# One decoder block on one core: other early transfers and ranks, a stored order, and the scores' low-part product on 64 rows

## The chip, the cores and the metric

The kernel runs on one core of one Trainium2 chip. Its time is the device time in microseconds (us) of one execution of the program, given as the median of several. Five engines share the work: TensorE (PE, with its weight load PEld shown apart), VectorE (DVE), ScalarE (ACT), GpSimd (POOL) and SyncE (SP), which here issues every DMA.

## The reference

One decoder block on x of 256 tokens by 1024 features, with 256 memory tokens, all in float32:

```python
h = rmsnorm(x, g_pre_mix); z = h @ w_in
q_nsa, kv_nsa, g_nsa, qkv_ml, if_ml, o_ml, q_mem, g_merge = split(z)
# 1 sparse attention: 16 heads of 64 in 4 groups of 4 that share keys and values
o_cmp, p_cmp = nsa_compressed(...)      # keys of 32-token blocks through a small MLP
o_slc = nsa_selected(...)               # top 16 blocks of 64 keys: at 256 tokens all four
o_win = nsa_window(...)                 # window of 512: at 256 tokens plain causal attention
y_nsa = gb[0] * o_cmp + gb[1] * o_slc + gb[2] * o_win
# 2 mLSTM, 4 heads of 128, with a causal convolution
y_ml = sigmoid(o_ml) * headnorm(mlstm_chunkwise(q_m, k_m, v_m, i_pre, logf))
# 3 cross-attention to the memory, 4 heads of 128
y_mem = memory_xattn(q_mem, mem, g_mem, w_mem_kv)
y = sum(sigmoid(g_merge[b]) * (y_b @ w_proj_b))
x = x + rmsnorm(y @ w_out, g_post_mix)
x = x + rmsnorm((silu(gate) * up) @ w_ffn_down, g_post_ffn)   # gate, up = rmsnorm(x) @ w_ffn_in
```

## The kernel before, in words

**How a product is made.** Every float32 operand of a large product is split into a high part (rounded to the reduced format float32r) and a low part (the rest): ACT copies the high part, DVE subtracts it (`split`). A product is then three matmuls, high by high, high by low, low by high (`mm3`). Weights come in units of 128 x 1024 (512 KB) from one array `in_W` in the order in which the kernel fetches them (`fetch`): each lands in a tile `raw`, of which ACT makes `whi` and DVE `wlo`. Four buffers each of `raw`, `whi` and `wlo` rotate.

**The stages**, in program order: the memory keys (matmuls into the PSUM tiles `pd`, with `mh` and `ml`, the scaled memory `memt` split in two); the memory values (into `pss`); the root mean square norms, for which squares (`msq` of the memory, `sq` of x, whose transpose arrives as `xt`) are added on DVE and summed over the partitions by matmuls with a column of ones (`col`), and spread again (`rbc`); the normalised x as `hh` and `hl`; the sparse attention's keys and values; their compression (`ph`, with two weight tiles `w1` of 1 MB); the gates, transposed by `pg`; the mLSTM (small products `pa`, `psm`, `pm`); the memory attention; the eight halves of the sparse attention (four groups, two blocks of 128 tokens), between which the merge gates and other projections are laid as filling; the merge; the output projection `w_out`; and the feed-forward network. At the end of `w_out` its result is scaled into `xg`, transposed (`ptx`), and split into `xc`, from which the feed-forward products (`pss<-wq,xc`) start.

**Scores.** `nsa_half(g, tb, qs, yT)` works on one group and one block of tokens, in two pairs of heads. The query tile `qs` holds a head's high part in one half of the 128 partitions and its low part in the other half; for the heads j = 0 and 1 of a pair the halves are exchanged. The key tiles `kh` and `kl` (both parts of the tile `kk`) hold the keys' high and low part, alike in both halves. So one matmul with `kh` on 128 rows gives both query parts times the high keys, and one with `kl` adds the low keys. A third, in bf16, adds the mask (`identb` with `msk`). The result is the tile `sc`; DVE takes maxima (`mx`), ACT exponentials.

**What sets the order.** The code above does not run directly: `Plan` records every operation with its dependencies, and each gets a number in order of recording. `schedule` (line 276 and on) then lists the operations by simulated times with given costs: the next one of an engine is the ready one of lowest rank, which is its number, less a `boost` of its own, and plus what `plan.later(n)` added where it was recorded. Then `choose` tries 12 settings of two costs and 40 random changes of the boosts, counts each order with `replay`, and keeps the shortest. `issue` (line 511) emits the operations in that order, so every instruction of the profile has the line L511.

Of the kernel before, what the change touches and what calls it, by code (L numbers as in the profile page):

```python
# [33 lines left out]

C_Q, C_KV, C_G, C_ML, C_IF, C_O, C_QM, C_MG = 0, 1024, 2560, 2608, 4144, 4152, 4664, 5176


K_ID, K_TRI, K_RV, K_BM, K_M0, K_C1, K_MT, K_END = 0, 128, 256, 257, 261, 533, 549, 677
# [127 lines left out]
class Plan:  # L166
# [67 lines left out]
    def cost(op):  # L234
# [7 lines left out]
        if op.dma:  # L242
            return math.prod(views[0].shape) * 4 / 330.0
        if op.eng == "PE":
            dtype = op.a[1].dtype
            op.load = 56.0 if dtype == BF16 else 109.0
            if op.method == "transpose":
                return n / 1.2 + 2
            if dtype == F32:
                return max(262.0, n / 0.6 + 10)  # L250
            return n / 2.4 + (2.5 if dtype == BF16 else 13.3) + (100 if op.a[1].shape[0] <= 32 else 0)
# [20 lines left out]
    START, TABLE, ISSUE, LAND = 570.0, 1283.0, 460.0, 1700.0  # L272
# [179 lines left out]
    MATMUL, SLACK, ROUNDS = (2.0, 6.0, 10.0, 13.3), (0.0, 60.0, 130.0), 40  # L452

    def choose(self):


        for op in self.ops:
            op.users = []
        for op in self.ops:
            for d in op.deps:  # L460
                d.users.append(op)
        best = None
        for matmul in self.MATMUL:
            for slack in self.SLACK:
                order = self.schedule(matmul, slack, {})
                length = self.replay(order)
                if best is None or length < best[0]:
                    best = length, matmul, slack, {}
        length, matmul, slack, boost = best
        rng = random.Random(0)  # L470
        stale = True
        for _ in range(self.ROUNDS):
            if stale:
                order = self.schedule(matmul, slack, boost)
                self.replay(order)
                waits = [(op.lost, op) for op in order if op.eng == "PE" and op.lost > 90 and op.why]
                chains = []
                for lost, op in waits:
                    chain, d = [], op.why
                    while d is not None and len(chain) < 16:  # L480
                        chain.append(d.i)
                        d = d.why or max((x for x, strict in d.deps.items() if strict), key=lambda x: x.end,
                                         default=None)
                    chains.append(chain)
                stale = False
            if not waits:
                break
            chain = rng.choices(chains, [w[0] for w in waits])[0]
            step = rng.choice((20, 50, 100, 200, 400))
            new = dict(boost)  # L490
            for i in chain[:rng.choice((1, 2, 4, 8, 16))]:
                new[i] = new.get(i, 0) + step
            trial = self.replay(self.schedule(matmul, slack, new))
            if trial <= length:
                length, boost, stale = trial, new, True
        self.chosen = length, matmul, slack, boost
        return self.schedule(matmul, slack, boost)
# [17 lines left out]
def block_kernel(ctx, tc, order, xN, xT, memT, cst, vec, row, wg, w1, w2, W, out):  # L515
# [35 lines left out]
    def ps_t(shape, name="pt"):  # L551
        return psum.tile(shape, F32, tag="t", bufs=2, name=name)
# [150 lines left out]
    rw = one.tile([P, 520], F32, name="rw")  # L703
    wgt = work.tile([P, 8, 64], F32, tag="p", bufs=2, name="wgt")
    w2t = one.tile([P, 192], F32, name="w2t")
# [5 lines left out]
    for u in range(4):  # L711
        if u < FINE:
            raw = fetch(("mem_k", u), lambda h: dma(out=memt[:, 2 * u + h, :], in_=memT[:, 2 * u + h, :]))
            del ready["mem_k", u]
            w = [wpool.tile([P, 1024], F32R, tag=t, bufs=4, name=t) for t in ("whi", "wlo")]
            for h in range(2):
                c = slice(512 * h, 512 * h + 512)
                mem_in(2 * u + h)
                split(w[0][:, c], w[1][:, c], raw[:, c])
        else:  # L720
            dma(out=memt[:, 2 * u:2 * u + 2, :], in_=memT[:, 2 * u:2 * u + 2, :])
            mem_in(2 * u)
            mem_in(2 * u + 1)
            w = unit(("mem_k", u))
        for k in (2 * u, 2 * u + 1):
            for j in range(4):
                b = slice(512 * (k % 2) + P * j, 512 * (k % 2) + P * j + P)
                mm3(kps[j // 2][:, j % 2, :], w[0][:, b], w[1][:, b], mh[:, k, :], ml[:, k, :],
                    k == 0 and j % 2 == 0, k == KD - 1 and j % 2 == 1, skip_group_check=True)
    fetch(("mem_v", 0))  # L730
    fetch(("mem_v", 1))
    for h in range(2):
        dma(out=xt[:, 4 * h:4 * h + 4, :], in_=xT[:, 4 * h:4 * h + 4, :])
    dma(out=cs[:, 0:P], in_=cst[:, 0:P])
    msq = [work.tile([P, 4, S], F32, tag="p", bufs=2, name="msq") for _ in range(2)]
# [34 lines left out]
    fetch(("kv", 0))  # L770
    fetch(("kv", 1))
# [4 lines left out]
    dma(out=rw, in_=bass.AP(tensor=row.tensor, offset=row.offset, ap=[[0, P], [1, 520]]))  # L776
    dma(out=w2t, in_=w2)
# [7 lines left out]

    w1t = []
    for j in range(2):
        t = bigt("G", 3, [P, 16, P], F32, f"w1_{j}")
        w1t.append(t)
        dma(out=t, in_=w1[j].rearrange("p (a n) -> p a n", a=16))  # L790
# [301 lines left out]
    def nsa_half(g, tb, qs, yT):  # L1092
# [4 lines left out]
        for pr in range(2):  # L1097
# [4 lines left out]
            for j in range(2):  # L1102
                q = qs[:, 2 * pr + j, t]
                if tb == 0:
                    s = ps_s([P, 512], "sc")
                    PE.matmul(s[:, 0:272], q, kh[:, g, P:400], start=True, stop=False)
                    PE.matmul(s[:, 0:272], q, kl[:, g, P:400], start=False, stop=False)
                    PE.matmul(s[:, 0:272], identb, M0, start=False, stop=True)
                    sc = (s[:, P:144], s[:, 0:P], s[:, 144:272])
                else:  # L1110
                    s, s2 = ps_s([P, 512], "sc"), ps_s([P, 512], "sc")
                    for x, c, n in ((s, 0, 272), (s2, 272, 256)):
                        PE.matmul(x[:, 0:n], q, kh[:, g, c:c + n], start=True, stop=False, skip_group_check=True)
                        PE.matmul(x[:, 0:n], q, kl[:, g, c:c + n], start=False, stop=False, skip_group_check=True)
                    PE.matmul(s[:, 0:P], identb, MD, start=False, stop=False, skip_group_check=True)
                    PE.matmul(s[:, 256:272], identb, MC1, start=False, stop=True, skip_group_check=True)
                    PE.matmul(s2[:, P:256], identb, MD, start=False, stop=True, skip_group_check=True)
                    sc = (s[:, 256:272], s[:, 0:256], s2[:, 0:256])
                for b in range(3):
                    DVE.tensor_reduce(mx[:, j, b:b + 1], sc[b], axis=AX.X, op=ALU.max, negate=True)  # L1120
                for b in range(3):
                    out = pc[:, 2 * pr + j, :] if b == 0 else pv4[:, j, b - 1]
                    exps.append(ACT.activation(out, sc[b], AF.Exp, bias=mx[:, j, b:b + 1],
                                               accum_out=sm[:, j, b:b + 1]))
# [94 lines left out]
    for t, i in ((g1, 520), (gp[:, 0, :], 520 + 2 * D), (go, 520 + D)):  # L1219
        dma(out=t, in_=bass.AP(tensor=row.tensor, offset=row.offset + i, ap=[[0, P], [1, D]]))  # L1220
# [33 lines left out]
    for tb, r in scaled("w_out", (yh, yl), 4, ((gp[:, 1, :], zg), (g1, [z[:, 0, :], z[:, 1, :]])),  # L1254
                        (1.0 / D, 1.0 / D), (1.0, 1.0)):
        rs_.append(r)
        for q in range(2):
            c = slice(512 * q, 512 * q + 512)
            DVE.scalar_tensor_tensor(xg[:, tb, c], zg[tb][:, c], r, xg[:, tb, c], op0=ALU.mult, op1=ALU.add)
            pt = ps_t([P, 4, P], "ptx1")  # L1260
            for j in range(4):
                PE.transpose(pt[:, j, :], xg[:, tb, (4 * q + j) * P:(4 * q + j + 1) * P], ident)
            t = slice(tb * P, (tb + 1) * P)
            split(xh[:, 4 * q:4 * q + 4, t], xl[:, 4 * q:4 * q + 4, t], pt)
# [64 lines left out]
def _layout(inputs):  # L1329
# [56 lines left out]
    w2 = np.concatenate([w2k, w2k, a["cmp_w2_v"][0]], axis=1)  # L1386
    row = np.concatenate([a[n] for n in ("ml_head_g", "ml_gate_b", "g_post_mix", "g_post_ffn", "g_pre_ffn")], axis=1)
# [19 lines left out]
    arrs = {"xN": a["x"][0], "xT": xT, "memT": memT, "cst": cst, "vec": vec, "row": row, "wg": wg, "w1": w1, "w2": w2}  # L1407
# [32 lines left out]
```

## Time and profile before

| | us |
|---|---|
| median of 3 runs | 552.94 |
| lowest and highest | 551.5, 555.01 |
| the profiled execution's own time | 552.94 |
| its span in the profile | 551.1 |
| what lies around the span | 1.84 |

A row of an engine's time line gives start and length in us, engine, operation, the tile written and the tiles read (out<-in), and the shape: for a matmul the rows and columns of the weights, then the moving tile, then the count (x3: three alike one after the other, shown as one row). A bracket says how long the engine had been idle and which instruction ended that. TensorE's instructions are pipelined, so that the length of one is longer than the distance to the next one's start; distances of starts tell what one costs. The granted clock is the share of TensorE's full speed that the throttle granted.

### The profile page before, as it was taken

To read this page: it belongs to the slowest core of one execution; us is meant where nothing else is said; L and a number is where in the kernel's file an instruction comes from. 1 tells how busy PE (TensorE), PEld (TensorE's weight loads), DVE (VectorE), ACT (ScalarE), POOL (GpSimd) and SP (SyncE) were. 2 spreads that over 40 slices of the span, in tenths; PEclk is the share of its full clock that TensorE was granted. 3 is DMA by queue.
4 is the path that set the end of the run, shared out by engine and by line. 5 is a ranking of instruction groups with operands and counts; after the bars stand their busy time and mean duration, and the time that the engine had idled before them with its cause. 6 is when DMAs were issued, how large, how long until landed. Compare 5 with 4: busy or idle time off the path is not lost.

```text
span 551.1 us, 8728 instructions
## 1 busy us (share of the span) xinstructions
PE 539.2 (98%) x3164; PEld 472.0 (86%) x3164; DVE 422.5 (77%) x813; ACT 342.7 (62%) x672; POOL 20.5 (4%) x34
## 2 busy tenths in 40 slices
PE   8899999999999999999999999999999999999995
PEld 8789999998989889889888888778888888888884
DVE  4797697589899897996888687975778787854543
ACT  6755777574699776875896444764666666643430
POOL 0010000000000100100100000000000000000000
PEclk9899999999999999999999999999999999999998
DMA  7966336734633354255254656753555555565512
GB/s 264 312 261 230 118 113 185 233 120 132 213 111 118 119 189 152 80 170 210 88 182 160 217 196 196 235 180 121 175 189 184 191 185 186 189 192 191 191 72 76
DMA packets 29419, 95.45 MB, mean 173 GB/s; under 512 B 3392, under 2 KB 6720, under 8 KB 29120
## 3 DMA queue, kind: packets, MB, share of 16 engines
q1 hardware_dynamic: 29376, 94.89, 52.0%
q8 instruction: 25, 0.41, 0.3%
q14 instruction: 18, 0.15, 0.1%
HBM read 92.78 MB, written 1.05 MB: 170 GB/s over the span
## 4 chain that ended last, share of the span: by engine, by line
PE 92%; DVE 3%; DMA 2%; issue 1%; ACT 1%; SPq 0%; DVEq 0%; ACTq 0%
PE pd L511 49%; PE pss L511 29%; PE sc L511 3%; PE pvn L511 2%; PE ptn L511 2%; PE ph L511 2%; DMA memt<-in_memT 1%; DMA raw<-in_W 1%; DVE wlo L511 1%; PE pn L511 1%; DVE wq L511 1%; PE psm L511 1%; DVE z L511 1%; PE pvm L511 1%; PE pq L511 1%
## 5 line engine op out<-in xcount | busy, mean ns | idle before, releaser
L511 DVE TENSOR_TENSOR wlo<-raw,whi 128x1024 fp32r<-128x1024 f32 (+1 forms) x161 | 193.6, 1206 | 66.7 <-ACT whi L511 63.3
L511 ACT ACTIVATE whi<-raw 128x1024 fp32r<-128x1024 f32 (+1 forms) x161 | 167.6, 1044 | 101.6 <-PE pd L511 57.0
L511 PE MATMUL pd<-hh,whi 128*128 128x256 f32 x224 | 64.3, 287 | 0.0
L511 PE MATMUL pd<-hh,wlo 128*128 128x256 f32 x224 | 64.1, 286 | 0.0
L511 PE MATMUL pd<-hl,whi 128*128 128x256 f32 x224 | 63.7, 285 | 0.2 <-DVE hl L511 0.2
L511 PE MATMUL pd<-whi,hh 128*128 128x512 f32 x144 | 58.8, 409 | 0.0
L511 PE MATMUL pd<-wlo,hh 128*128 128x512 f32 x144 | 58.3, 405 | 0.0
L511 PE MATMUL pd<-whi,hl 128*128 128x512 f32 x144 | 56.8, 397 | 0.0
L511 PEld LDWEIGHTS pd<-hl,whi 128*128 128x128 f32 x224 | 42.8, 191 | 0.6 <-DVE hl L511 0.4
L511 PE MATMUL pss<-xc,whi 128*128 128x512 f32 x168 | 43.2, 392 | 0.0
L511 PEld LDWEIGHTS pd<-hh,whi 128*128 128x128 f32 x224 | 42.8, 191 | 0.4 <-ACT hh L511 0.2
L511 PEld LDWEIGHTS pd<-hh,wlo 128*128 128x128 f32 x224 | 42.8, 191 | 0.2
L511 PE MATMUL pss<-whi,u 128*128 128x512 f32 x132 | 42.4, 392 | 0.0
L511 PEld LDWEIGHTS pss<-xc,whi 128*128 128x128 f32 x168 | 30.7, 189 | 5.4
L511 PE MATMUL pd<-xc,whi 128*128 128x512 f32 x120 | 31.9, 394 | 0.0
L511 PEld LDWEIGHTS pd<-whi,hl 128*128 128x128 f32 x144 | 27.1, 188 | 4.8
L511 PEld LDWEIGHTS pd<-whi,hh 128*128 128x128 f32 x144 | 27.2, 189 | 4.3
L511 PEld LDWEIGHTS pd<-wlo,hh 128*128 128x128 f32 x144 | 27.3, 189 | 3.9
L511 PEld LDWEIGHTS pss<-whi,u 128*128 128x128 f32 x132 | 24.8, 188 | 5.5
L511 ACT ACTIVATE pp<-sc,mx 128x128 f32<-128x128 f32 (+1 forms) x64 | 26.9, 433 | 1.4 <-DVE mx L511 1.4
L511 PE MATMUL pss<-wlo,u 128*128 128x512 f32 x66 | 25.9, 392 | 0.0
L511 DVE TENSOR_REDUCE mx<-sc 128x1 f32<-128x16 f32 (+2 forms) x96 | 22.3, 288 | 4.0 <-PE sc L511 3.8
(324 smaller groups left out, 1115.4 us busy)
## 6 DMA issues: line engine op xcount, KB each, us to landing
raw<-in_W SPq DMA_DIRECT2D x159, 512.0 KB, 4.2
w<-in_w SPq DMA_DIRECT2D x2, 1024.0 KB, 6.6
raw<-in_W SPq DMA_DIRECT2D x6, 256.0 KB, 4.0
xt<-in_xT SPq DMA_DIRECT2D x2, 512.0 KB, 8.5
kk<-kk SPq DMA_DIRECT2D x8, 128.0 KB, 4.7
x<-in_xN SPq DMA_DIRECT2D x2, 512.0 KB, 3.8
out<-z SPq DMA_DIRECT2D x8, 128.0 KB, 2.0
memt<-in_memT SPq DMA_DIRECT2D x6, 128.0 KB, 3.9
```

The source lines that it names most:

```text
L511: op.ins_ = getattr(op.real, op.method)(*map(arg, op.a), **{k: arg(x) for k, x in op.kw.items()})
```

## The change

The change consists of several edits, none of which alters what is computed, with one exception: the low keys are no longer multiplied with the queries' low part.

1. **The order is stored.** `choose` no longer searches; it schedules with a fixed table of boosts (`BOOST`) and two fixed costs, `MATMUL` 13.3 and `SLACK` 130. Some costs of the planner are others: a DMA's bytes over 410 plus 70 ns instead of over 330, its landing 2000 instead of 1700 ns, and a float32r matmul with 64 rows is counted with half the time per column.
2. **Early transfers.** `xt` is fetched ahead of the memory-value weights, the units 2 and 3 of these and the first four units of the keys and values are fetched earlier, and the `w1` tiles use other buffers. The constants `rw` and `w2t` become columns of the tile `cs` (two DMAs fewer), and the gains `row` arrive in memory already spread over the 128 partitions.
3. **Ranks.** `plan.later(tb * 100 - 100)` stands around the end of `w_out`.
4. **Scores.** In `nsa_half` the products of both heads with `kh` are recorded first, then both with `kl`, each on the 64 rows that hold its head's high part, then the masks.

```diff
+BOOST = {
+    0: 9970, 2: 370, 14: 700, 15: 400, 18: 16410, 19: 5900, 20: 400, 88: 20, 94: 20, 95: 20, 97: 20, 122: 20, 127:
...
+MATMUL, SLACK = 13.3, 130.0
...
-            return math.prod(views[0].shape) * 4 / 330.0
+            return math.prod(views[0].shape) * 4 / 410.0 + 70
...
-            return n / 2.4 + (2.5 if dtype == BF16 else 13.3) + (100 if op.a[1].shape[0] <= 32 else 0)
+            return (n / (4.8 if op.a[1].shape[0] == 64 and dtype == F32R else 2.4) + (2.5 if dtype == BF16 else 13.3)
+                    + (100 if op.a[1].shape[0] <= 32 else 0))
...
-    START, TABLE, ISSUE, LAND = 570.0, 1283.0, 460.0, 1700.0
+    START, TABLE, ISSUE, LAND = 570.0, 1283.0, 460.0, 2000.0
...
+        order = self.schedule(MATMUL, SLACK, BOOST)
+        self.chosen = self.replay(order), MATMUL, SLACK, BOOST
+        return order
...
-    rw = one.tile([P, 520], F32, name="rw")
+    rw = cs[:, K_RW:K_RW + 520]
+    w2t = cs[:, K_W2:K_W2 + 192]
...
+    for h in range(2):
+        dma(out=xt[:, 4 * h:4 * h + 4, :], in_=xT[:, 4 * h:4 * h + 4, :])
     fetch(("mem_v", 0))
     fetch(("mem_v", 1))
-    for h in range(2):
-        dma(out=xt[:, 4 * h:4 * h + 4, :], in_=xT[:, 4 * h:4 * h + 4, :])
     dma(out=cs[:, 0:P], in_=cst[:, 0:P])
+    for u in (2, 3):
+        fetch(("mem_v", u))
+    fetch(("kv", 0))
+    fetch(("kv", 1))
+    w1t = []
+    for j, tg in enumerate("CV"):
+        t = bigt(tg, 1, [P, 16, P], F32, f"w1_{j}")
+        w1t.append(t)
+        dma(out=t, in_=w1[j].rearrange("p (a n) -> p a n", a=16))
+    fetch(("kv", 2))
+    fetch(("kv", 3))
...
+            def scores(c, n, marks):
+                ss = [ps_s([P, 512], "sc") for _ in range(2)]
+                for j in range(2):
+                    PE.matmul(ss[j][:, 0:n], qs[:, 2 * pr + j, t], kh[:, g, c:c + n], start=True, stop=False,
+                              skip_group_check=True)
+                for j in range(2):
+                    r = slice(64 * j, 64 * j + 64)
+                    PE.matmul(ss[j][:, 0:n], qs[r, 2 * pr + j, t], kl[r, g, c:c + n], start=False, stop=False,
+                              skip_group_check=True)
+                for j in range(2):
+                    for i, (c0, m) in enumerate(marks):
+                        PE.matmul(ss[j][:, c0:c0 + m.shape[1]], identb, m, start=False, stop=i == len(marks) - 1,
+                                  skip_group_check=True)
+                return ss
...
-        for q in range(2):
-            c = slice(512 * q, 512 * q + 512)
-            DVE.scalar_tensor_tensor(xg[:, tb, c], zg[tb][:, c], r, xg[:, tb, c], op0=ALU.mult, op1=ALU.add)
...
+        with plan.later(tb * 100 - 100):
+            for q in range(2):
+                c = slice(512 * q, 512 * q + 512)
+                DVE.scalar_tensor_tensor(xg[:, tb, c], zg[tb][:, c], r, xg[:, tb, c], op0=ALU.mult, op1=ALU.add)
```

What the order of instructions is then, at the three places that the prediction speaks of (the start, the end of `w_out`, the scores). At the start, SP, which issues the transfers; `raw` are weights (the 128x512 ones and the first 128x1024 one are the memory keys'), `cs` constants. Before:

```order
L511 DMA memt<-in_memT 128x256
L511 DMA raw<-in_W 128x512
L511 DMA xt<-in_xT 128x1024
L511 DMA memt<-in_memT 128x512
L511 DMA raw<-in_W 128x1024 x3
L511 DMA xt<-in_xT 128x1024
L511 DMA cs<-in_cst 128x128
```

and after:

```order
L508 DMA memt<-in_memT 128x256 x2
L508 DMA raw<-in_W 128x512 x2
L508 DMA memt<-in_memT 128x512
L508 DMA raw<-in_W 128x1024
L508 DMA xt<-in_xT 128x1024 x2
L508 DMA raw<-in_W 128x1024 x2
L508 DMA cs<-in_cst 128x128
```

The first half of `xt` moved behind the last memory-key weights, and the second half ahead of the memory-value weights.

Also at the start, TensorE at the change from the memory keys (`pd`) to the memory values (`pss`), before:

```order
L511 MATMUL pd<-mh,wlo 128x256
L511 MATMUL pss<-whi,mh 128x512
L511 MATMUL pss<-wlo,mh 128x512
L511 MATMUL pss<-whi,ml 128x512
L511 MATMUL pss<-whi,mh 128x512
```

and after:

```order
L508 MATMUL pd<-mh,wlo 128x256
L508 MATMUL col<-ones,msq 128x1 x2
L508 MATMUL col<-ones,sq 128x1 x2
L508 MATMUL pss<-whi,mh 128x512 x2
L508 MATMUL rbc<-cs,rm 128x128 x2
L508 MATMUL pss<-wlo,mh 128x512
```

The sums over the squares of the memory (`msq`) and of x (`sq`) moved ahead of the first memory-value matmul.

TensorE at the end of `w_out`, with `ptx` the transposes of its result. Before:

```order
L511 MATMUL pd<-wlo,yh 128x512
L511 MATMUL pd<-whi,yl 128x512
L511 MATMUL ptx_4160<-cs,xg 128x128 [waits DVE_49,PE_49]
L511 MATMUL ptx_4160<-cs,xg 128x128 x3
L511 MATMUL ptx_4167<-cs,xg 128x128 [waits DVE_49,PE_49]
L511 MATMUL ptx_4167<-cs,xg 128x128 x3
L511 MATMUL pss<-wq,xc 128x512 [waits Activation_49]
```

and after:

```order
L508 MATMUL ptx_4143<-cs,xg 128x128 [waits DVE_49,PE_49]
L508 MATMUL ptx_4143<-cs,xg 128x128 x3
L508 MATMUL pd<-whi,yh 128x512
L508 MATMUL ptx_4150<-cs,xg 128x128 [waits DVE_49,PE_49]
L508 MATMUL ptx_4150<-cs,xg 128x128 x3
L508 MATMUL pd<-wlo,yh 128x512
L508 MATMUL pd<-whi,yl 128x512
L508 MATMUL pd<-whi,yh 128x512
L508 MATMUL pd<-wlo,yh 128x512
L508 MATMUL pd<-whi,yl 128x512
L508 MATMUL pss<-wq,xc 128x512 [waits Activation_49]
```

The transposes of the first block of tokens moved ahead by six matmuls of the projection.

TensorE at the scores, here the first pair in the program, where at most places a head's product with `kh`, its product with `kl` and its mask still stand together, as they did before:

```order
L508 MATMUL pd<-hl,whi 128x256
L508 MATMUL sc<-kk,qs 128x272 [waits DVE_49,Activation_49]
L508 MATMUL sc<-kk,qs 128x272 [waits DMAHW6_49,DMAHW4_49]
L508 LDWEIGHTS identb
L508 MATMUL sc<-msk,identb 128x272
L508 MATMUL sc<-kk,qs 128x272 x2
L508 LDWEIGHTS identb
L508 MATMUL sc<-msk,identb 128x272
L508 MATMUL pd<-hh,wlo 128x256
```

Of the 24 pairs of `kl` products, 6 stand directly one behind the other; the other 36 products stand between a 128-row product and a mask.

More of the change, by code (lines that the diff above doesn't have):

```diff
@@ L32 @@
 NEG = -1e30
+BOOST = {
[25 rows of a table added]
+}
+MATMUL, SLACK = 13.3, 130.0
 C_Q, C_KV, C_G, C_ML, C_IF, C_O, C_QM, C_MG = 0, 1024, 2560, 2608, 4144, 4152, 4664, 5176
-K_ID, K_TRI, K_RV, K_BM, K_M0, K_C1, K_MT, K_END = 0, 128, 256, 257, 261, 533, 549, 677
+K_ID, K_TRI, K_RV, K_BM, K_RW, K_W2, K_M0 = 0, 128, 256, 257, 261, 781, 973
+K_C1, K_MT, K_END = K_M0 + 272, K_M0 + 288, K_M0 + 416
 V_PRE, V_MEM, V_PM, V_PF, V_PO, V_CW, V_CB, V_PEK, V_PEV, V_END = 0, 8, 16, 24, 32, 40, 72, 80, 96, 112
@@ L450, in replay @@
         return max(op.end for op in order)
-    MATMUL, SLACK, ROUNDS = (2.0, 6.0, 10.0, 13.3), (0.0, 60.0, 130.0), 40
     def choose(self):
@@ L461, in choose @@
                 d.users.append(op)
[L462 to L497, printed above, removed]
+        order = self.schedule(MATMUL, SLACK, BOOST)
+        self.chosen = self.replay(order), MATMUL, SLACK, BOOST
+        return order
     def issue(self):
@@ L514, in block_kernel @@
 @with_exitstack
-def block_kernel(ctx, tc, order, xN, xT, memT, cst, vec, row, wg, w1, w2, W, out):
+def block_kernel(ctx, tc, order, xN, xT, memT, cst, vec, row, wg, w1, W, out):
     plan = Plan(tc)
@@ L701, in keep_k @@
         split(kmem[:, 0, 2 * i:2 * i + 2, :], kmem[:, 1, 2 * i:2 * i + 2, :], kt)
-    rw = one.tile([P, 520], F32, name="rw")
+    rw = cs[:, K_RW:K_RW + 520]
+    w2t = cs[:, K_W2:K_W2 + 192]
     wgt = work.tile([P, 8, 64], F32, tag="p", bufs=2, name="wgt")
-    w2t = one.tile([P, 192], F32, name="w2t")
     dma(out=vc, in_=vec)
@@ L769, in block_kernel @@
                                      op0=ALU.mult, op1=ALU.subtract)
-    fetch(("kv", 0))
-    fetch(("kv", 1))
     dma(out=wgt, in_=wg)
@@ L775, in block_kernel @@
     dma(out=mraw, in_=cst[:, K_M0:])
-    dma(out=rw, in_=bass.AP(tensor=row.tensor, offset=row.offset, ap=[[0, P], [1, 520]]))
-    dma(out=w2t, in_=w2)
     identb = one.tile([P, P], BF16, name="identb")
@@ L783, in block_kernel @@
     M0, MC1, MT, MD = msk[:, 0:272], msk[:, 272:288], msk[:, 288:416], msk[:, 0:P]
[L786 to L790, printed above, removed]
     hid = one.tile([P, 2, NG, 32], F32, name="hid")
@@ L1101, in nsa_half @@
             pv4 = pp[:, 0:512 * nkb].rearrange("p (h b n) -> p h b n", h=2, b=2)
[L1102 to L1124, printed above, removed]
@@ new lines, in softmax @@
+            def softmax(j, b, s):
+                DVE.tensor_reduce(mx[:, j, b:b + 1], s, axis=AX.X, op=ALU.max, negate=True)
+                out = pc[:, 2 * pr + j, :] if b == 0 else pv4[:, j, b - 1]
+                exps.append(ACT.activation(out, s, AF.Exp, bias=mx[:, j, b:b + 1], accum_out=sm[:, j, b:b + 1]))
+            if tb == 0:
+                ss = scores(P, 272, ((0, M0),))
+                for j in range(2):
+                    for b, c in enumerate((slice(P, 144), slice(0, P), slice(144, 272))):
+                        softmax(j, b, ss[j][:, c])
+            else:
+                ss = scores(0, 272, ((0, MD), (256, MC1)))
+                for j in range(2):
+                    for b, c in enumerate((slice(256, 272), slice(0, 256))):
+                        softmax(j, b, ss[j][:, c])
+                ss = scores(272, 256, ((P, MD),))
+                for j in range(2):
+                    softmax(j, 2, ss[j][:, 0:256])
@@ L1218, in block_kernel @@
     gp = bigt("G", 3, [P, 2, D], F32, "gp")
-    for t, i in ((g1, 520), (gp[:, 0, :], 520 + 2 * D), (go, 520 + D)):
-        dma(out=t, in_=bass.AP(tensor=row.tensor, offset=row.offset + i, ap=[[0, P], [1, D]]))
+    for i, t in enumerate((g1, gp[:, 0, :], go)):
+        dma(out=t, in_=row[i])
     xg = bigt("G", 3, [P, 2, D], F32, "xg")
@@ L1256, in block_kernel @@
         rs_.append(r)
-        for q in range(2):
-            c = slice(512 * q, 512 * q + 512)
-            DVE.scalar_tensor_tensor(xg[:, tb, c], zg[tb][:, c], r, xg[:, tb, c], op0=ALU.mult, op1=ALU.add)
[L1260 to L1264, printed above, removed]
+        with plan.later(tb * 100 - 100):
+            for q in range(2):
+                c = slice(512 * q, 512 * q + 512)
+                DVE.scalar_tensor_tensor(xg[:, tb, c], zg[tb][:, c], r, xg[:, tb, c], op0=ALU.mult, op1=ALU.add)
+                pt = ps_t([P, 4, P], "ptx1")
+                for j in range(4):
+                    PE.transpose(pt[:, j, :], xg[:, tb, (4 * q + j) * P:(4 * q + j + 1) * P], ident)
+                t = slice(tb * P, (tb + 1) * P)
+                split(xh[:, 4 * q:4 * q + 4, t], xl[:, 4 * q:4 * q + 4, t], pt)
     wq = [bigt(tg, n, [P, 2, 1024], F32R, "wq") for tg, n in (("Y", 2), ("Y", 2), ("V", 1), ("E", 2))]
@@ L1385, in _layout @@
         pe("cmp_pe_k"), pe("cmp_pe_v")], axis=1)
-    w2 = np.concatenate([w2k, w2k, a["cmp_w2_v"][0]], axis=1)
-    row = np.concatenate([a[n] for n in ("ml_head_g", "ml_gate_b", "g_post_mix", "g_post_ffn", "g_pre_ffn")], axis=1)
+    row = np.stack([np.broadcast_to(a[n], (P, D)) for n in ("g_post_mix", "g_pre_ffn", "g_post_ffn")])
     wg = np.zeros((D, 64), np.float32)
@@ L1406, in _layout @@
     cst[:, K_BM:K_BM + 4] = (i[:, None] % 64 // 16) == np.arange(4)[None, :]
-    arrs = {"xN": a["x"][0], "xT": xT, "memT": memT, "cst": cst, "vec": vec, "row": row, "wg": wg, "w1": w1, "w2": w2}
+    cst[:, K_RW:K_RW + 512] = a["ml_head_g"]
+    cst[:, K_RW + 512:K_RW + 520] = a["ml_gate_b"]
+    cst[:, K_W2:K_M0] = np.concatenate([w2k, w2k, a["cmp_w2_v"][0]], axis=1)
+    arrs = {"xN": a["x"][0], "xT": xT, "memT": memT, "cst": cst, "vec": vec, "row": row, "wg": wg, "w1": w1}
     return {k: np.ascontiguousarray(v) for k, v in arrs.items()}, units
```

24 rows, old and new, of the table BOOST are left out of this document.

## The prediction

> **What bounds the kernel now.** I read the page first (busy shares, then the chain), then TensorE's waits, then a table by stretch, and last the single instructions at the places where TensorE stood still.
>
> ```profile
> span 551.1 us, 8728 instructions
> PE 539.2 (98%) x3164; PEld 472.0 (86%) x3164; DVE 422.5 (77%) x813; ACT 342.7 (62%) x672; POOL 20.5 (4%) x34
> PE 92%; DVE 3%; DMA 2%; issue 1%; ACT 1%; SPq 0%; DVEq 0%; ACTq 0%
> ```
>
> TensorE (PE) is busy 98% of the span and carries 92% of the chain that ends last. A change can therefore save only what TensorE loses, about 12 us in all with the start and the tail, or shorten its own work. A microsecond added to TensorE's stream is a microsecond of time.
>
> ```profile
> PE pd L511 <- ACT whi L511: 1.1, 1, 1.1
> PE pd L511 <- DVE wlo L511: 0.7, 1, 0.7
> PE pss L511 <- ACT xc L511: 0.5, 1, 0.5
> PE pss L511 <- DVE xc L511: 0.4, 1, 0.4
> ```
>
> In TensorE's list of waits (total us, times, longest) nothing is over 1.1 us, and these come once each. The first two are in the first stage, the memory keys; the last two are where the output projection hands over to the feed-forward network. No row of the list names a DMA, and none lies between 46 and 357 us, where TensorE is busy for 311.00 us of 311.00:
>
> ```profile
> 46.00:357.00 311.00, 311.00 (x1947) 275.49 (x1947) 259.27 (x566) 212.29 (x467) 14.24 (x14) 1.00 0.49 161
> ```
>
> ```profile
> 0.00:8.00 8.00, 5.85 (x28) 5.39 (x29) 2.54 (x5) 4.99 (x9) 1.18 (x10) 1.00 0.70 218
> 8.00:15.70 7.70, 7.70 (x66) 7.70 (x65) 5.01 (x10) 5.67 (x11) 0.00 (x0) 1.00 0.95 351
> 15.70:18.50 2.80, 1.03 (x7) 0.62 (x6) 2.49 (x3) 2.17 (x3) 0.00 (x0) 1.00 1.02 402
> 18.50:22.50 4.00, 4.00 (x21) 4.00 (x22) 3.78 (x7) 2.73 (x4) 0.00 (x0) 0.57 0.85 265
> 22.50:35.40 12.90, 12.90 (x66) 10.79 (x65) 10.93 (x21) 7.37 (x11) 1.80 (x2) 1.00 0.70 242
> ```
>
> Here a row is a stretch: its length, busy time of PE, PEld, DVE, ACT and POOL, granted clock, DMA share, GB/s. From 15.7 to 18.5 TensorE works 1.03 of 2.80 us while the DMA engines are full. After that pause the granted clock falls to 0.57 for 4 us, and 4 us at 0.57 do the work of 2.3: the pause costs another 1.7 us. From 22.5 on TensorE is full at full clock.
>
> **The start.** The early transfers change order: the last 512 KB of memory-key weights are no longer behind 512 KB of `xt`, while the first memory-value weights are now behind all of `xt`.
>
> ```profile
> 15.64 0.28 PE L511 MATMUL pd<-mh,wlo 128*128 128x256 f32 x1
> 16.98 0.39 PE L511 MATMUL pd<-mh,whi 128*128 128x256 f32 x1 [1.06 <-ACT whi L511]
> 17.44 0.28 PE L511 MATMUL pd<-ml,whi 128*128 128x256 f32 x1
> 18.43 0.39 PE L511 MATMUL pd<-mh,wlo 128*128 128x256 f32 x1 [0.71 <-DVE wlo L511]
> 22.37 0.45 PE L511 MATMUL pss<-whi,mh 128*128 128x512 f32 x1
> 20.75 1.68 ACT L511 ACTIVATE sq<-xt 128x512 f32<-128x512 f32 x3
> 15.88 1.99 ACT L511 ACTIVATE whi<-raw 128x1024 fp32r<-128x1024 f32 x2
> ```
>
> The matmuls of this stage start 0.11 to 0.12 us apart, so of the 1.34 us from 15.64 to 16.98 and the 0.99 us from 17.44 to 18.43, 2.1 us are loss. The transfers run at 351 to 402 GB/s, so 512 KB fewer ahead bring the last weights some 1.3 to 1.5 us earlier, and with them `whi` (1.0 us each on ACT) and `wlo`. That takes most of the 2.1 us, and if the clock stays up also the 1.7: at best −3.8.
>
> What is late next is the sum of squares. In the new order TensorE's rows `col<-msq` and `col<-sq` stand directly behind the last memory-key matmul and ahead of the first memory value; before, `pss` stood there and `col<-sq` came much later. `col<-sq` needs all of `xt`, four squares of 0.56 us each on ACT, and the additions on DVE. Before, the squares' second half starts behind 20.75. The new order has 4.2 MB up to the end of `xt`; by 15.7 us the queue had moved 8.0 × 218 + 7.7 × 351 KB = 4.4 MB, so `xt` lands at 15 to 17. With `msq`, `mh` and one `whi` ahead of the squares on ACT, four squares and three additions, I estimate `col` at 20 to 21.5 us, while the memory keys are through at 22.6 − 3.8 = 18.8. So a pause of about 1.3 us returns at this place, and the value products `pss` stand behind it on TensorE. I take **−2.5 us** (−3.8 and 1.3 back). The ends are −3.8 (no pause) and +0.5 (the pause is longer and the clock is lowered again).
>
> [...]
>
> **The output projection.**
>
> ```profile
> 356.53 0.39 PE L511 MATMUL pd<-whi,yl 128*128 128x512 f32 x1
> 356.76 1.03 PE L511 MATMUL ptx<-cs,xg 128*128 128x128 f32 x8
> 358.28 0.73 PE L511 MATMUL pss<-wq,xc 128*128 128x512 f32 x2 [0.49 <-ACT xc L511]
> 359.38 0.50 PE L511 MATMUL pss<-wq,xc 128*128 128x512 f32 x1 [0.36 <-DVE xc L511]
> 356.37 2.35 DVE L511 TENSOR_TENSOR wlo<-raw,whi 128x1024 fp32r<-128x1024 f32 x2
> ```
>
> Eight transposes end at 357.8 and the feed-forward matmuls wait for `xc`: 0.49 on ACT, then 0.36 on DVE, which did two `wlo` (2.35 us) first. Now six `pd` matmuls, 0.23 us apart as at 356.53, stand behind the first four transposes (1.4 us of cover for both waits), and DVE does one `wlo` less ahead of `xc`. I take **−0.8**, ends −1.2 (the starts show 0.5 and 0.7 us lost around them) and 0 (the cover only brings another weight late). The other new ranks lie in stretches without a wait: 0, with 1 either way. The two fewer DMAs and the wider `row` are hidden by a queue that TensorE nowhere waits for: 0; were a weight late, it would cost about what the longest wait above does, 1.1.
>
> **The scores.** This is the largest term. There are 96 products with the keys, 48 of them with the low parts, in 24 pairs. Before, each is a matmul on 128 rows between others on 128 rows. Now it has the 64 rows with the query's high part; the low part's half is left out.
>
> ```profile
> L511 PE MATMUL sc<-kk,qs x96: 274/287/392, 111.8 to 279.0; 128*128 128x272 f32 x64, 128*128 128x256 f32 x32
> 111.79 0.41 PE L511 MATMUL sc<-kk,qs 128*128 128x272 f32 x2
> 112.04 0.29 PE L511 MATMUL sc<-msk,identb 128*128 128x272 bf16 x1
> ```
>
> The two products at 111.79 take 0.25 us to the mask at 112.04, so one starts 0.12 to 0.13 us behind another. A 64-row product streams as many columns, so alone it isn't shorter. Only the two of a pair could run side by side. But in the new order 36 of the 48 stand alone between a 128-row product and the 128-row mask, and only 6 pairs are left together: 42 excursions into the 64-row mode.
>
> ```profile
> 55.59 0.41 DVE L511 TENSOR_TENSOR gts<-gts,pgf 64x256 f32<-64x256 f32 x1
> 56.16 0.28 PE L511 MATMUL pd<-hl,whi 128*128 128x256 f32 x1
> 56.37 0.33 PE L511 MATMUL pg<-cs,gts 64*128 64x64 f32 x2
> 56.63 0.39 PE L511 MATMUL pd<-hh,wlo 128*128 128x256 f32 x1
> 56.86 0.28 PE L511 MATMUL pd<-hh,whi 128*128 128x256 f32 x1
> ...
> 62.67 0.28 PE L511 MATMUL pd<-hl,whi 128*128 128x256 f32 x1
> 62.78 0.38 PE L511 MATMUL pa<-cs,As 128*4 128x128 f32 x2
> 62.92 0.36 PE L511 MATMUL pd<-hh,wlo 128*128 128x256 f32 x1
> 63.12 0.28 PE L511 MATMUL pd<-hh,whi 128*128 128x256 f32 x1
> ...
> 56.37 0.20 PEld L511 LDWEIGHTS pg<-cs,gts 64*128 64x128 f32 x2
> 56.63 0.19 PEld L511 LDWEIGHTS pd<-hh,wlo 128*128 128x128 f32 x1
> 62.89 0.19 PEld L511 LDWEIGHTS pd<-hh,wlo 128*128 128x128 f32 x1
> ```
>
> The kernel has one 64-row operation now, the gate transposes `pg`, in the middle of a dense `pd` stream. From the `pd` ahead to the second `pd` behind it take 0.70 us (56.16 to 56.86). The same figure around `pa`, two small matmuls on 128 rows with 4 columns, is 0.45 us (62.67 to 63.12). The excess of **0.25 us** is the price of entering and leaving. The load rows show it: the weights of `pg` load only when `pg` starts, and those of the following `pd` when it starts (both at 56.63), whereas around `pa` the load (62.89) begins ahead of its matmul (62.92). It is no wait for data: `gts` was done at 56.00.
>
> The sum: 36 lone products at 0.25 are 9.0. Six pairs at 0.25, less one stream of 0.12 each if the halves overlap, are 0.8. Together **+9.8**. Below, the term is bounded by no price for the switch: −0.7 with 6 overlapped pairs. Above, by 48 excursions at 0.25, +12. I stay near the upper end, since `pg` is the only row with 64 rows and the load behind it is exposed too.
>
> [...]
>
> **Sum.** −2.5 − 0.8 + 9.8 = +6.5. The profiled execution took 552.94 us, its span of 551.1 and 1.84 around it, and it is also the median of the three runs: **559.4 us**. What a measurement of this kernel can tell from no change is about 1%, 5.5 us: under 547.4 is faster, over 558.5 slower.
>
> **Rivals.**
> - The halves cost nothing to enter and run side by side where they stand together; the start gains fully. For it: `pg` transposes plain f32 and is no product in reduced f32, so some of the 0.25 may not carry over. Against it: the exit behind `pg` (56.63 to 56.86, 0.23 us for a `pd` that takes 0.12) waits for nothing and is slow too. −0.7 (to −2.9) − 3.8 − 0.8: 545.5 to 547.6, about 547.0.
> - No price for the switch, but the start gains only −2.5 and nothing overlaps: 552.94 − 3.3 = 549.6, no change.
> - The other side, sharper than the forecast: the pause at `col<-msq` and `col<-sq` lowers the granted clock again. Its price is the 1.7 us of the stretch at 0.57 on top of the 1.3 us pause, and the start gives −0.8 instead of −2.5: 561.1. It decides if TensorE works less than about 1.03 in 2.8 us there. For it: ACT and DVE must do the squares ahead of the value weights. Against: `xt` comes some 4 us earlier.
> - The pair does not do what it says: the scheduler separates 18 of 24 pairs. That is certain from the order, and in the forecast already. It leaves the saving at a quarter even where the switch is free.
>
> **How the numbers follow.** A price for the switch near `pg`'s has 0.70: 0.50 for the forecast and 0.20 for the clock lowered again. Free switching has 0.30: 0.15 for the first rival and 0.15 for the second. Around the forecast the switch may be 0.20 to 0.28 us (8 to 11 us in all) and the start −3.8 to 0: 556.5 to 562, about 0.55 of it over 558.5. The clock rival lies over 558.5 for 0.8 of its share. Slower: 0.28 + 0.16 = 0.44. Faster: 0.7 of the first rival and some of the second, 0.13. The same: 0.43. The range of 8 in 10 must leave out no more than the lower half of the first rival and the tip of the upper ones: **546.8 to 562.5**. The likeliest case's own range is 556.5 to 562.
>
> **What would show it.** Right: TensorE's rows around a lone 64-row product take 0.25 us more than around its 128-row neighbours; the median spacing from `kk` high to the mask is some 0.35 to 0.4 us instead of 0.13 to 0.15; the memory keys end near 19 us; a pause shows at `col`; and no wait over 0.3 us stands at `pss<-wq,xc`. Wrong: the weights of a 64-row product load during the product ahead of it; or the two of a pair start within 0.02 us with all else unchanged; or the new order leaves a wait in the dense middle, where I put none.

## The result, and the profile after

The changed kernel takes 560.51 us median (558.45 to 561.25), the kernel before 552.22 in the same comparison: a ratio of 1.0133, with a 95% interval of 1.0107 to 1.0159. The forecast was 559.4. In some executions of the kernels here, and not in others, TensorE's granted clock is 0.50 for some 3.4 us near the start (from 19.1 to 22.5 us in the profiled execution of before, nowhere in that of after), which makes some 1.3 to 2 us (3.4 us at 0.50 lose 1.7), so that these two executions differ by 5.5 us (552.94 and 558.45), and the medians by 8.3.

The page of the changed kernel (span, busy shares, chain):

```profile
span 556.7 us, 8747 instructions
PE 546.6 (98%) x3164; PEld 470.8 (85%) x3164; DVE 422.5 (76%) x813; ACT 345.1 (62%) x673; POOL 21.4 (4%) x34
PE 95%; DMA 2%; DVE 1%; issue 1%; SPq 0%; ACT 0%; POOL 0%; DVEq 0%; ACTq 0%
```

TensorE has as many instructions as before (3164) and 7.4 us more busy time; DVE is where it was. The time went into TensorE's own stream, not into waits. Its waits (total us, times, longest):

```profile
PE pd L508 <- DVE wlo L508: 0.7, 1, 0.7
PE pd L508 <- ACT mh L508: 0.6, 1, 0.6
PE rbc L508 <- POOL rm L508: 0.6, 1, 0.6
PE col L508 <- DVE sq L508: 0.5, 1, 0.5
```

The two waits at `pss<-wq,xc` are gone, and two have come at the sums of squares (`col`, and `rbc`, which spreads them), where the forecast put a pause. TensorE at the scores:

```profile
110.27 0.28 PE L508 MATMUL pd<-hl,whi 128*128 128x256 f32 x1
110.39 0.61 PE L508 MATMUL sc<-kk,qs 128*128 128x272 f32 x2
110.93 0.29 PE L508 MATMUL sc<-msk,identb 128*128 128x272 bf16 x1
110.97 0.69 PE L508 MATMUL sc<-kk,qs 128*128 128x272 f32 x2
111.59 0.29 PE L508 MATMUL sc<-msk,identb 128*128 128x272 bf16 x1
111.63 0.37 PE L508 MATMUL pd<-hh,wlo 128*128 128x256 f32 x1
```

Each `sc<-kk,qs` row holds a head's product with the high keys (128 rows) and its product with the low keys (64 rows; the row shows the first one's shape). To the mask they take 0.54 us (110.39 to 110.93), where before it was 0.25 (111.79 to 112.04): 0.29 more per head. A product with the low keys and the load of its weights, first in the changed kernel, then the second head's in the version of it with all rows put back (the first experiment below):

```profile
110.60 0.18 PEld L508 LDWEIGHTS sc<-kk,qs 64*128 64x128 f32 x1
110.61 0.39 PE L508 MATMUL sc<-kk,qs 64*128 64x272 f32 x1
...
110.50 0.19 PEld L508 LDWEIGHTS sc<-kk,qs 128*128 128x128 f32 x1
110.62 0.28 PE L508 MATMUL sc<-kk,qs 128*128 128x272 f32 x1
```

The 64-row weights load only when their product starts, as those of `pg` did; the 128-row weights load 0.12 us ahead of theirs, during the matmul before. The mask's load tells nothing here: it begins with the mask in the kernel before too (112.03 and 112.04). All 96 products together, before 287 ns in the median:

```profile
L508 PE MATMUL sc<-kk,qs x96: 276/378/393, 109.4 to 286.6; 128*128 128x272 f32 x32, 64*128 64x272 f32 x32, 128*128 128x256 f32 x16, 64*128 64x256 f32 x16
```

The start, by stretch (length, busy time of PE, PEld, DVE, ACT, POOL, granted clock, DMA share, GB/s):

```profile
15.70:18.50 2.80, 1.91 (x14) 1.70 (x14) 2.80 (x7) 1.93 (x5) 0.00 (x0) 1.00 1.02 406
18.50:22.50 4.00, 3.02 (x23) 2.50 (x21) 3.86 (x10) 3.27 (x4) 1.59 (x1) 1.00 0.65 259
```

TensorE's pause has not gone but spread: 0.9 us from 15.7 to 18.5 and 1.0 from 18.5 to 22.5, without a lower clock in this execution. DVE is full in both stretches (2.80 of 2.80, 3.86 of 4.00).

### The profile page after: what moved, and what is told of

Its sections match the earlier page's. It is cut to its first block, busy times and chain, and to the rows that moved or that the text cites. A ratio compares the mean times of both kernels' runs of the same rounds, so it can differ in the third digit from the quotient of the medians.

```text
span 556.7 us, 8747 instructions
## 1 busy us (share of the span) xinstructions
PE 546.6 (98%) x3164; PEld 470.8 (85%) x3164; DVE 422.5 (76%) x813; ACT 345.1 (62%) x673; POOL 21.4 (4%) x34
## 4 chain that ended last, share of the span: by engine, by line
PE 95%; DMA 2%; DVE 1%; issue 1%; SPq 0%; ACT 0%; POOL 0%; DVEq 0%; ACTq 0%
PE pd L508 50%; PE pss L508 29%; PE sc L508 5%; PE pvn L508 2%; PE ptn L508 2%; PE ph L508 1%; DMA memt<-in_memT 1%; DMA raw<-in_W 1%; PE pn L508 1%; PE ptx L508 1%; PE psm L508 1%; PE pvm L508 1%; PE pq L508 0%; DVE sq L508 0%; SPq L508 0%
## 5 line engine op out<-in xcount | busy, mean ns | idle before, releaser
L508 DVE TENSOR_REDUCE mx<-sc 128x1 f32<-128x16 f32 (+2 forms) x96 | 23.1, 290 | 10.3 <-PE sc L508 9.7
L508 ACT ACTIVATE pp<-sc,mx 128x256 f32<-128x256 f32 (+1 forms) x64 | 26.7, 427 | 1.7 <-DVE mx L508 1.6
L508 PE MATMUL sc<-kk,qs 128*128 128x272 f32 (+2 forms) x96 | 27.5, 348 | 0.0
```

What stands on the lines that cost most here:

```text
L508: op.ins_ = getattr(op.real, op.method)(*map(arg, op.a), **{k: arg(x) for k, x in op.kw.items()})
```

## The experiments

**The scores.** Theory A: entering and leaving the 64-row mode costs about 0.28 us, and the opposite halves of a pair run side by side. Theory B: the rearranged order makes the scores late. First, the order kept and the rows put back:

```diff
-                    PE.matmul(ss[j][:, 0:n], qs[r, 2 * pr + j, t], kl[r, g, c:c + n], ...)
+                    op = PE.matmul(ss[j][:, 0:n], qs[r, 2 * pr + j, t], kl[r, g, c:c + n], ...)
+                    op.a = (op.a[0], qs[:, 2 * pr + j, t], kl[:, g, c:c + n])   # what is emitted
```

> The changed kernel with its order of instructions word for word, but each product with the low keys again on 128 rows. Theory A (entering and leaving the 64-row mode costs the time; 36 lone products at 0.28 us and 6 pairs at 0.16 by the rows of the changed kernel): 9.9 us less than the changed kernel in the stretch of the scores, so about 550.5 us median, 2 to 3 under the kernel before, with 0.13 us between the starts of a head's three score matmuls. Theory B (the rearranged order, heads interleaved and ranks from the table, makes the scores late; the rows don't matter): no more than 1 us less than the changed kernel, about 560.

Measured: 549.38 us (548.16 to 550.98), 11.1 under the changed kernel, and 0.9945 (0.9925 to 0.9965) of before. TensorE at the same two heads:

```profile
110.12 0.41 PE L508 MATMUL sc<-kk,qs 128*128 128x272 f32 x2
110.37 0.29 PE L508 MATMUL sc<-msk,identb 128*128 128x272 bf16 x1
110.41 0.50 PE L508 MATMUL sc<-kk,qs 128*128 128x272 f32 x2
110.75 0.29 PE L508 MATMUL sc<-msk,identb 128*128 128x272 bf16 x1
```

0.25 us to the mask again. Since nothing else differs, theory B falls. The two profiled executions, both at the full granted clock throughout (0.997 and 0.998 in the mean of the span), have spans of 556.7 and 546.4 us, 10.3 apart, which is the better measure of the rows than the 11.1 of the medians. The opposite edit, in the kernel before:

```diff
-                        PE.matmul(x[:, 0:n], q, kl[:, g, c:c + n], start=False, stop=False, ...)
+                        op = PE.matmul(x[:, 0:n], q, kl[:, g, c:c + n], start=False, stop=False, ...)
+                        r = slice(64 * j, 64 * j + 64)
+                        op.a = (op.a[0], qs[r, 2 * pr + j, t], kl[r, g, c:c + n])
```

> The kernel before with its order word for word, but each product with the low keys on the 64 rows that hold its head's high part. There all 48 products stand alone between a 128-row product and a mask. Theory A: 48 x 0.28 = 13.5 us more than before, about 566. Theory B: the same as before within 1 us, about 552.5.

Measured: 565.98 us, a ratio of 1.0263 (1.0237 to 1.0288), 12.9 more than before (553.04 in that comparison). 48 excursions at 0.28 are 13.4. So the price holds in either order.

Then the pairs put together by a dependency of the scheduler:

```diff
-                    PE.matmul(ss[j][:, 0:n], qs[:, 2 * pr + j, t], kh[:, g, c:c + n], ...)
+                    both = PE.matmul(ss[j][:, 0:n], qs[:, 2 * pr + j, t], kh[:, g, c:c + n], ...)
...
-                    PE.matmul(ss[j][:, 0:n], qs[r, 2 * pr + j, t], kl[r, g, c:c + n], ...)
+                    PE.matmul(ss[j][:, 0:n], qs[r, 2 * pr + j, t], kl[r, g, c:c + n], ..., after=(both,))
```

> The changed kernel, where each product with the low keys of a pair must wait in the list of the scheduler for the second product with the high keys, so that all 24 pairs stand together instead of 6. Some fillings move with it. Theory A: 24 excursions at 0.16 us instead of 36 at 0.28 and 6 at 0.16: 3.8 us instead of 11, so 6 to 7 under the changed kernel, about 553.5, 1.5 either way for the moved fillings. A rival C (two 64-row products of one pair run side by side only where nothing else is ready, 3 ns apart by chance of six): no gain from standing together, 48 x 0.28, about 563.

Measured: 556.94 us, 1.0093 (1.0066 to 1.0121) of before: 3.6 under the changed kernel by the medians (2.2 by the two ratios to before), not 6 to 7. By the trace 22 of the 24 pairs stand together; two are still apart. A pair itself is as theory A has it:

```profile
145.81 0.28 PE L508 MATMUL pd<-hh,wlo 128*128 128x256 f32 x1
146.02 0.39 PE L508 MATMUL sc<-kk,qs 64*128 64x272 f32 x2
146.34 0.32 PE L508 MATMUL sc<-msk,identb 128*128 128x128 bf16 x4
...
163.44 0.39 PE L508 MATMUL pvn<-pTl,vs 128*128 128x256 f32 x1 [0.97 <-DVE pTl L508]
167.11 0.39 PE L508 MATMUL pd<-hh,whi 128*128 128x256 f32 x1 [1.23 <-DVE on L508]
```

Both 64-row products together are done in 0.32 us (146.02 to 146.34), as long as a lone one takes (321 ns in the median of the changed kernel). Much of what was missing is in the last two rows: waits of 0.97 and 1.23 us that the changed kernel doesn't have. The first head's low product now waits for the second head's high one; that its softmax is later for it, and TensorE out of filling there, is my reading and was not tried by itself. Rival C falls by the rows; its time (563) too.

Whether the halves make the overlap: the same order with both products on the rows 0 to 63.

```diff
...
+                    op.a = (op.a[0], qs[0:64, 2 * pr + j, t], kl[0:64, g, c:c + n])
```

> As the kernel with all 24 pairs together, in the same order, but both products of a pair on the rows 0 to 63 (for the second head the low part of the queries times the low keys, so part of the low-key term is left out). Theory A with the halves as the cause of the overlap: the second product starts 0.11 to 0.22 us behind the first instead of 0.003, so 3 to 5 us more than with opposite halves, about 557.5. If any two 64-row products overlap: the same time.

Measured: 558.85 us (1.0139, 1.0107 to 1.0171), 1.9 more than with opposite halves, less than the 3 to 5 expected.

```profile
147.57 0.28 PE L508 MATMUL pd<-hh,wlo 128*128 128x256 f32 x1
147.78 0.52 PE L508 MATMUL sc<-kk,qs 64*128 64x272 f32 x2
148.23 0.32 PE L508 MATMUL sc<-msk,identb 128*128 128x128 bf16 x4
```

The pair takes 0.45 us to the mask, not 0.32: 0.13 more, one stream (24 x 0.13 = 3.1; the medians show 1.9, and the intervals of the two overlap, so that the rows carry this and not the time). Of the two waits above, this profile has the 0.97 us and not the 1.23, about what the time falls short by. The expectation of up to 0.22 more was too high; that the second load lies beside the first product is my reading of the 0.13. So opposite halves do run side by side, and the saving per pair is 0.13 us. Last, each pair's two products run twice in one excursion (a single execution, 558.0 us):

> The version with all pairs together, and each pair's two low-key products run twice in the same excursion (the low-key term counts double in the result). Theory A (the price is for entering and leaving; inside, a pair costs one stream): the second pair starts 0.22 us behind the first (its load counts once, as in the same-half rows), the mask 0.22 behind the second, 24 x 0.12 = 3 us more than with one pair. Rival F (a product on 64 rows streams slowly, 0.3 us each): 24 x 0.3 = 7 us more.

```profile
143.46 0.28 PE L508 MATMUL pd<-hh,wlo 128*128 128x256 f32 x1
143.67 0.39 PE L508 MATMUL sc<-kk,qs 64*128 64x272 f32 x2
143.90 0.29 PE L514 MATMUL sc<-kk,qs 64*128 64x272 f32 x2
144.12 0.32 PE L508 MATMUL sc<-msk,identb 128*128 128x128 bf16 x4
```

Four products in two halves take 0.45 us, as long as two in one half: inside the mode a pair costs one stream, and rival F (slow streaming) falls. From 143.46 to 144.12 are 0.66 us; on 128 rows it would be the `pd` at 0.12 and four products at 0.13, 0.64. **Break-even, by this estimate, is a little over two pairs per excursion** (no run has three); the changed kernel has one pair in 6 excursions and half a pair in 36.

**The start.** SP's order alone, in the kernel before: both halves of `xt` issued directly behind the last memory-key weights (moved in the finished list; the other engines' orders word for word as before).

> The kernel before with its order on every engine word for word, except that SP issues both halves of x directly behind the last memory-key weights and ahead of the value weights, as the changed kernel does. Theory A (512 KB of x ahead of the last key weights make the pause at 15.7 us): the keys end 1.3 to 1.5 us earlier or more where the clock stays up, but the value weights land 2.5 us later, so the first value matmul gains only 1 to 2: about 551.5 median. Rival E (the start is bound by ACT and DVE, not by the transfers): no change, 553.

Measured: 552.23 us, 1.0003 (0.9987 to 1.002) of before: no change, as rival E had it, and theory A's 1 to 2 us did not come.

```profile
20.28 0.28 PE L519 MATMUL pd<-mh,wlo 128*128 128x256 f32 x1
21.46 0.49 PE L519 MATMUL pss<-whi,mh 128*128 128x512 f32 x1 [0.90 <-ACT whi L519]
22.72 0.51 PE L519 MATMUL pss<-wlo,mh 128*128 128x512 f32 x1 [0.77 <-DVE wlo L519]
```

The first value matmul waits 0.90 us for its own weights, and the next 0.77. It is not rival E's reason: ACT had stood idle for 3.93 us until the first of these weights landed, so the transfers do bind here. In the kernel before with 64-row scores, which has the old transfers and the same order here, it came without a wait:

```profile
20.71 0.39 PE L511 MATMUL pss<-whi,mh 128*128 128x512 f32 x1
20.93 0.39 PE L511 MATMUL pss<-wlo,mh 128*128 128x512 f32 x1
```

So the keys' last matmul at 20.28 is only some 0.3 us earlier than there, and the values are later (21.46 against 20.71): what was pulled ahead of one stage pushed the next one back. Then the other way round, the version with full rows with the value weights fetched ahead of x (`fetch(("mem_v", 0))` and `("mem_v", 1)` stand above the two DMAs of `xt`):

> The version with full rows, but the first two units of the memory-value weights are fetched ahead of the two halves of x, as in the kernel before; the other early transfers stay. TensorE's order then has the value matmuls directly behind the keys again and the sums of squares later. Theory A (the pause at the sums of squares is the price of x ahead of the values): the 1.5 us of pauses between 19.8 and 22.6 us go, about 548 median. Rival D (the same time is lost later, where the normalised x waits for its sum): the stage of hh starts no earlier than 34.0 us, 549.4 or more.

Measured: 550.82 us, 0.9977 (0.9961 to 0.9994) of before, 1.4 more than e1_full_rows. The pauses at the sums of squares went; this came:

```profile
36.55 0.28 PE L508 MATMUL pd<-hh,whi 128*128 128x256 f32 x1
38.87 0.38 PE L508 MATMUL pd<-hh,wlo 128*128 128x256 f32 x1 [2.04 <-DVE wlo L508]
```

Theory A's gain was taken back 17 us later, as rival D said, though not by its mechanism: the stage began earlier than 34.0 us (33.70) and waited for the weights' low parts on DVE, not for the norm.

**The output projection.** The version with full rows with `plan.later(0)` for `plan.later(tb * 100 - 100)`:

> The version with full rows (e1_full_rows) without the later rank at the end of the output projection: the first eight transposes stand together again behind all of the projection's matmuls, the rest of the order is the same. Theory A (the six matmuls behind the transposes cover the two waits for the split): the pauses of 0.5 and 0.7 us ahead of the first feed-forward matmuls come back, +1.2 us, about 550.6 median, and both rows show in TensorE's waits. Rival (the other weights' splits moved on DVE, and that alone took the pause away): no pause, 549.4.

Measured: 549.88 us, 0.9954 (0.9937 to 0.9972), against 0.9945 with the rank: medians 0.5 apart, which the intervals don't separate. The waits are back:

```profile
PE pss L508 <- ACT xc L508: 0.5, 1, 0.5
PE pss L508 <- DVE xc L508: 0.4, 1, 0.4
```

By the spans of the two profiled executions (547.3 and 546.4) the rank is worth 0.9 us. The sign is shown by the rows, the size to a few tenths only.

**The stored order.** Full rows and the search of before instead of the table:

> The version with full rows, but with the search of the kernel before in place of the stored table (under the changed planner's costs, a product with the low keys counted as one on 128 rows). The orders differ in about a hundred rows, most of them in the first 20 us. Theory A (what is gained comes from the transfers and the ranks at the output projection, which both orders have): the same as e1_full_rows, 549.4 within 1 us. Rival G (the table itself gains): 2 us or more above it, 551.5.

Measured: 550.03 us, 0.9964 (0.9944 to 0.9985). The table gains nothing that can be told from the search. And the whole change without the 64 rows, the planner's cost included (`n / 2.4` for all):

> The version with full rows where the planner also counts those products as on 128 rows; the stored table stays, so this is the whole change without the 64 rows. Theory A: 549.4 within 1 us, 10.5 to 11.5 under the changed kernel, about 0.5% faster than before. If the order of the scores mattered: more than 1 us off.

Measured: 550.43 us, 0.9965 (0.995 to 0.998), 10 under the changed kernel. With full rows the changed kernel is the best that was found: 0.35 to 0.55% under the kernel before in its three forms (e1_full_rows, g1_search_again, g2_full_cost).

## Why the prediction was right, and where it was not

- **What bounds the kernel** held. Between the changed kernel and e1_full_rows, which differ in the rows alone, TensorE's busy time differs by 10.3 us (546.6 and 536.3) and the span by 10.3 (556.7 and 546.4).
- **The scores** were the right term for the right reason: 42 excursions, the load of each 64-row product exposed (it begins 2 ns ahead of its product, in the median of the 48), `pg` the row to go by. The price is 0.28 to 0.29 us and not 0.25, and the term 10.3 by the spans (11.1 by the medians) and not 9.8. The 6 pairs overlap as the sum had it. One sign was worked out wrongly: from the high product to the mask I wrote 0.35 to 0.4 us; 0.25 as before and 0.25 on top would have been 0.50, and 0.54 was measured.
- **The start is the step that failed.** I took −2.5 from one execution of before in which the clock had been lowered, and put its 2.1 us of loss at the keys down to the order of the transfers. The kernel before with 64-row scores has word for word the same order up to the scores, and its profiled execution kept its clock. Its rows, then those of the changed kernel:

```profile
15.70:18.50 2.80, 2.29 (x19) 2.08 (x18) 2.69 (x3) 2.63 (x4) 0.00 (x0) 1.00 1.06 421
18.50:22.50 4.00, 4.00 (x30) 3.70 (x29) 3.78 (x7) 2.08 (x4) 0.00 (x0) 1.00 0.80 279
...
33.63 0.28 PE L511 MATMUL pd<-hh,whi 128*128 128x256 f32 x1
...
110.05 0.61 PE L511 MATMUL sc<-kk,qs 128*128 128x272 f32 x2
...
34.07 0.28 PE L508 MATMUL pd<-hh,whi 128*128 128x256 f32 x1
...
109.37 0.61 PE L508 MATMUL sc<-kk,qs 128*128 128x272 f32 x2
```

  With the old transfers TensorE loses 0.51 us in the first of these stretches, where it lost 1.77 in the profile of the prediction (2.1 by the starts), and `hh` starts at 33.63, against 35.36 there. With the new start and a full clock `hh` comes at 33.65 to 34.09 in four profiles (f3_pairs_twice, f1_no_later, the changed kernel, e1_full_rows), with as many matmuls ahead of it; with a clock lowered once it comes at 35.99 and 36.28 (g2_full_cost, e3_all_pairs), against the 35.36 of before. So at an even clock the new start gains nothing up to `hh`, though of the old order there is one profile only with a full clock and one with a lowered one. The keys' last matmul is 0.9 us earlier (19.72 against 20.59), and the pauses at the sums of squares, 0.48 and 0.58 us where I expected 1.3, and the sums themselves take that back. That the transfers alone give nothing is f4_before_x_moved.
- **Between `hh` and the scores** I forecast nothing, and there is a gain: 75.3 us in the changed kernel, 76.4 with the old order, whatever the clock at the start. Half of the 1.1 us are two waits of the kernel before that are gone; which edit took them away was not tried.

```profile
PE ph L511 <- issue: 0.3, 1, 0.3
PE pd L511 <- DVE hl L511: 0.2, 1, 0.2
```

- **The output projection**: −0.8 forecast, 0.5 (medians) to 0.9 (spans) shown, by the mechanism named.
- **The other ranks**: 0 forecast. Full rows stand at −3.0 us against before (0.0055 x 553, interval −4.1 to −1.9); 1.1 ahead of the scores and 0.9 or less at the output projection leave 1 us or a little more that lies in no one place of TensorE's rows. Which ranks give it was not tried.
- **The rivals.** Free switching is excluded by e1_full_rows and e2_before_64. The overlap of a pair is real (its two products start 3 ns apart and take 0.32 us together), but the first rival's −2.9, all 24 pairs overlapped at no price, is shown by no run: with 22 pairs together e3_all_pairs took 1.0093 of before, and the overlap was worth 0.13 us a pair. What lowers the clock stays open. The pauses of 0.48 to 0.59 us at the sums did not, in five profiles. In the three of the new order that have it, it falls between 18.7 and 19.1 us, ahead of those pauses, and in e4_same_half a second time at 25.6, behind a pause of 0.94 at `rbc` that the other two have without a second fall. Ahead of the first fall TensorE had worked little: 0.91 to 1.23 us from 15.7 to 18.5 in these three, 1.03 in before. But f2_values_first worked 0.98 there and kept its clock. In before and in these three TensorE had stood idle for no more than 1.4 us at a time ahead of the first fall. That the scheduler separates 18 of 24 pairs was certain; putting 22 together took back 2.2 to 3.6 us of the price, net of the waits that it brought.

That the time fell near the forecast is partly luck. The scores were 0.5 to 1.3 us dearer than forecast. The other terms came to −3.0 us in all against −3.3, but not where I put them: the start gave nothing of its −2.5, and gains of about 1 us each in two places that I had put at nothing stood in for it.

## What to carry to other kernels

Count the changes of row mode, not the rows saved: here a product on half the rows that stood alone in a dense stream cost 0.28 us more than the same on all rows, an excursion with one pair in opposite halves 0.16 more, and one with two pairs 0.02 more; by these numbers an excursion would pay from three pairs on, which is an estimate. This list scheduler separated what the source writes side by side (18 of 24 pairs), so look at the order before counting on an overlap. Before a gain at the start is taken from one execution, see in a second execution whether the granted clock and the waits there are the same.

## What the runs showed of the hardware that I had not expected

A lone 64-row product of 272 columns takes 0.32 us to the next 128-row one, two in opposite halves take 0.32 as well, two in the same half 0.45, and four in two halves 0.45. With 256 columns the lone one differs by 7 ns only (314 against 321 ns in the median between starts; 121 against 128 on 128 rows), so it is no slower stream but a fixed price, and it is the same ahead of a bf16 mask and ahead of an f32 product (318 ns in the kernel before with 64 rows).

The 0.28 us can be taken apart by medians of the same kind. Some 0.09 lie ahead of the product (218 ns from the high to the low product, against 127 on 128 rows). Some 0.10 lie between its start and the next one's: from a lone product to the mask are 321 ns, and from the second of two in the same half 217; that these go with its load, which begins 2 ns ahead of a lone product, is an estimate. The last 0.09 lie behind it (217 against 128).
